# Where the update of T in a blocked triangular inverse is summed: VectorE, or PSUM and ScalarE

## The chip, the cores and the metric

The kernel runs on one core of one Trainium2 chip. The metric is the device time of one execution in microseconds. The engines are TensorE (PE in the profile, its weight loads PEld), VectorE (DVE), ScalarE (ACT), GpSimd (POOL) and SyncE (SP, which here only issues DMAs). Each runs its own instruction list in order.

## The reference, cut to what matters

The program is a whole two-block network (a mixer block with gated DeltaNet and a state-space part, a convolutional feed-forward, then a recurrent and attention block with a mixture of experts). The change is in one piece of the gated delta rule (GDN). Per chunk of tokens, head and direction the reference solves a unit lower triangular system:

```
kk = jnp.einsum('bhnid,bhnjd->bhnij', kb, k) * decay
rhs = jnp.concatenate([v * beta[..., None], kb * jnp.exp(gc)[..., None]], axis=-1)
sol = lax.linalg.triangular_solve(kk, rhs, left_side=True, lower=True, unit_diagonal=True)
u, w = sol[..., :DV], sol[..., DV:]
...
def step(S, inp):
    u_c, w_c, qk_c, qd_c, kd_c, gl_c = inp
    v_new = u_c - jnp.einsum('bhcd,bhde->bhce', w_c, S)
    o_c = jnp.einsum('bhcd,bhde->bhce', qd_c, S) + jnp.einsum('bhij,bhje->bhie', qk_c, v_new)
    S = S * gl_c[..., None, None] + jnp.einsum('bhcd,bhce->bhde', kd_c, v_new)
    return S, o_c
```

## The kernel before

`phase_gdn` works on chunks of 128 tokens, ten chunks (eight of the sequence, two of the context) in two directions: 20 pairs (c, d), four heads each in one tile `[128, 4, 128]`. `prep(c, d, sl)` builds the inverse of a chunk's triangular matrix E. It starts from the identity and goes through seven levels, block sizes s = 1, 2, 4 ... 64 (`for l in range(7)`). T (`Tt`, float16) is the inverse so far, U (`Ut`) its transpose. One level is:

- L577: `pz` = Eh times the half of the columns of T that this level changes (view `Tv`): four matmuls of 64 columns, one for each head.
- L580, VectorE: `Z` = pz times the mask of the level.
- L593: `py` = Ut times Z, four matmuls of 64 columns (at level 0 Ut is the identity and Z itself is used).
- L594, VectorE: `Tv` = Tv minus py, reading PSUM and writing float16 back in place.
- L598 and L599: `put`, the changed rows of the transpose, by four matmuls, copied into `Ut` by ScalarE.

After the levels one refinement (`pn`, `R`, `pd`, L603 to L612) gives U. `step(c, d)` (L618 on) is the recurrence that uses it: float32 matmuls `pa`, `pb`, `pS`, `po`, `po2`, with VectorE (L629, L647, L668) and ScalarE (`vo` L637, `ot` L659) between them. `prep` also computes `pk` (L544) and `pq` (L558) in float32, and ScalarE's exponentials `D` (L502).

Five preps are in work at once (`NS = 5`), each with its own `Tt`, `Ut`, `Z`; the generators are advanced in turn, a part of each at a time. All PSUM results of the stage share seven banks (pool `psG`, tag `b`). The eighth bank is that of `zunits` (L706 on): 16 units of 48 float32r matmuls `zz` (L722), which compute the gates from the hidden states. `zunits` stands behind the GDN in the program, and `phase_ssd` behind it; the framework's scheduler, when the program is built, fixes the order of the instructions on each engine, and puts `zz` matmuls between those of the GDN where it finds room. What isn't done by the end of the GDN is done beside `phase_ssd`. Each half of a unit (24 matmuls) needs one load of 1 MB (`hx`, L719, issued by POOL) into one of two buffers, and a unit ends with a Silu on ScalarE (L725) and a store of `zd`, which the end of the next phase loads again (L877).

Of the kernel before, what the change touches and what calls it, by code (L numbers as in the profile page):

```python
# [10 lines left out]
F16 = mybir.dt.float16  # L11
# [3 lines left out]
AF = mybir.ActivationFunctionType  # L15
ALU = mybir.AluOpType
# [104 lines left out]
class K:  # L121
# [382 lines left out]
    def phase_gdn(self):  # L504
        nc, T = self.nc, self.T
# [6 lines left out]
        lv = self.pool("lvl", 1, ctx=st)  # L512
        lvl = lv.tile([128, 2, 7, 64], F32, name="lvl")
        nc.sync.dma_start(lvl, T["lvl"])
        I16 = lv.tile([128, 4, 128], F16, name="I16")
        nc.vector.tensor_copy(I16, self.I[:, None, :].to_broadcast([128, 4, 128]))
        ps = self.pool("psG", 7, PSUM, ctx=st)
        pr = self.pool("gprep", 2, ctx=st)
        ld = self.pool("gld", 3, ctx=st)
# [3 lines left out]
        def bank(name, dt=F32):  # L523
            return ps.tile([128, 4, 128], dt, name=name, tag="b")
# [4 lines left out]
        def cols(t, c):  # L529
            return t[:, :, c * 128:(c + 1) * 128]  # L530

        def prep(c, d, sl):
            kc = cols(self.kT, c)
            vt = ld.tile([128, 4, 128], F32, name="vt")
            nc.sync.dma_start(vt.rearrange("p h f -> p (h f)"), self.vtd[c])
            kt = ld.tile([128, 4, 128], F32, name="kt", bufs=5)
            nc.sync.dma_start(kt.rearrange("p h f -> p (h f)"), self.ktd[c])
            nc.gpsimd.tensor_tensor(kt, kt, self.erest[:, c, d, 0:4, None].to_broadcast([128, 4, 128]), op=ALU.mult)
            kt_[c, d] = kt
            D = ld.tile([128, 4, 128], F32, name="D")  # L540
            self.rows(D, c, d, 0)
            pk = bank("pk")
            for h in range(4):
                nc.tensor.matmul(pk[:, h, :], kc[:, h, :], kc[:, h, :], start=True, stop=True)  # L544
            yield
            self.expd(D, c, d, 0)
            yield
            E = pr.tile([128, 4, 128], F32, name="E")
            for h in range(4):
                nc.vector.scalar_tensor_tensor(E[:, h, :], pk[:, h, :], self.br2[:, c, d, h:h + 1], D[:, h, :],  # L550
                                               op0=ALU.mult, op1=ALU.mult)
            nc.gpsimd.affine_select(E, E, pattern=[[0, 4], [1, 128]], compare_op=ALU.not_equal, fill=1.0,
                                    base=0, channel_multiplier=-1)
            if c < 8:
                qc = cols(self.qT, c)
                pq = bank("pq")
                for h in range(4):
                    nc.tensor.matmul(pq[:, h, :], kc[:, h, :], qc[:, h, :], start=True, stop=True)  # L558
                P[c, d] = pr.tile([128, 4, 128], F32, name="P", bufs=5)
                nc.vector.tensor_mul(P[c, d], D, pq)  # L560
            yield
            Eh = pr.tile([128, 4, 128], F16, name=f"Eh{sl}", bufs=1)
            nc.scalar.copy(Eh, E)
            Tt = pr.tile([128, 4, 128], F16, name=f"Tt{sl}", bufs=1)
            nc.vector.tensor_copy(Tt, I16)
            Ut = pr.tile([128, 4, 128], F16, name=f"Ut{sl}", bufs=1)
            nc.gpsimd.tensor_copy(Ut, I16)
            yield
            for l in range(7):
                s = 1 << l  # L570
                Tv = Tt.rearrange("p h (n t s) -> p (h n) t s", t=2, s=s)[:, :, d, :]
                Uv = Ut.rearrange("p h (n t s) -> p (h n) t s", t=2, s=s)[:, :, 1 - d, :]
                Iv = I16[:, 0, :].rearrange("p (n t s) -> p n t s", t=2, s=s)[:, :, 1 - d, :]
                pz = ps.tile([128, 4, 64], F32, name="pz", tag="b")
                for h in range(4):
                    r = Tt[:, h, :].rearrange("p (n t s) -> p n t s", t=2, s=s)[:, :, d, :]
                    nc.tensor.matmul(pz[:, h, :].rearrange("p (n s) -> p n s", s=s), Eh[:, h, :], r,  # L577
                                     start=True, stop=True)
                Z = pr.tile([128, 4, 64], F16, name=f"Z{sl}", bufs=1)
                nc.vector.tensor_tensor(Z, pz, lvl[:, d, l, None, :].to_broadcast([128, 4, 64]), op=ALU.mult)  # L580
                if l == 0:
                    El = pr.tile([128, 4, 128], F16, name=f"El{sl}", bufs=1)
                    nc.gpsimd.tensor_tensor(El, E, Eh, op=ALU.subtract)
                    vh = sp.tile([128, 4, 128], F32, name="vh", bufs=5)
                    nc.gpsimd.tensor_tensor(vh, vt, self.rinv[:, c, :, None].to_broadcast([128, 4, 128]), op=ALU.mult)
                    vh_[c, d] = vh
                yield
                if l == 0:
                    y = Z
                else:  # L590
                    y = ps.tile([128, 4, 64], F32, name="py", tag="b")
                    for h in range(4):
                        nc.tensor.matmul(y[:, h, :], Ut[:, h, :], Z[:, h, :], start=True, stop=True)  # L593
                nc.vector.tensor_tensor(Tv, Tv, y.rearrange("p h (n s) -> p (h n) s", s=s), op=ALU.subtract)  # L594
                yield
                put = ps.tile([128, 4, 64], F32, name="put", tag="b")
                for h in range(4):
                    nc.tensor.matmul(put[:, h, :].rearrange("p (n s) -> p n s", s=s), Tt[:, h, :], Iv, start=True, stop=True)  # L598
                nc.scalar.copy(Uv, put.rearrange("p h (n s) -> p (h n) s", s=s))  # L599
                yield  # L600
            pn = bank("pn")
            for h in range(4):
                nc.tensor.matmul(pn[:, h, :], Eh[:, h, :], Tt[:, h, :], start=True, stop=False)  # L603
                nc.tensor.matmul(pn[:, h, :], El[:, h, :], Tt[:, h, :], start=False, stop=True)
            R = pr.tile([128, 4, 128], F16, name="R")
            nc.vector.tensor_tensor(R, Ibc, pn, op=ALU.subtract)
            yield
            pd = bank("pd")
            for h in range(4):
                nc.tensor.matmul(pd[:, h, :], R[:, h, :], Ut[:, h, :], start=True, stop=True)  # L610
            u = pr.tile([128, 4, 128], F32, name="U", bufs=4)
            nc.vector.tensor_tensor(u, Ut, pd, op=ALU.add)  # L612
            U[c, d] = u
# [66 lines left out]
        while ndone < len(order):  # L680
            for d in range(2):
                if cur[d] is None and chains[d] and (chains[d][0], d) in U:
                    cur[d] = step(chains[d].pop(0), d)
                if cur[d] is not None:
                    try:
                        next(cur[d])
                    except StopIteration:
                        cur[d] = None
                        ndone += 1
            rnd += 1  # L690
            if free and nprep < len(order) and nprep < ndone + 6 and rnd >= nxt:
                nxt = rnd + 4
                sl = free.pop(0)
                slots[sl] = prep(*order[nprep], sl)
                nprep += 1
            for sl in list(slots):
                try:
                    next(slots[sl])
                except StopIteration:
                    del slots[sl]  # L700
                    free.append(sl)
# [1522 lines left out]
```

## Time and profile before

| | us |
|---|---|
| median of 3 runs | 3375.71 (3370.09 to 3376.39) |
| the profiled execution | 3373.24 |
| its span | 3371.1 |
| PE busy in the span | 3088.8 (92%) |
| PEld, weight loads | 2327.3 (69%) |
| DVE busy | 1841.7 (55%) |
| ACT busy | 1171.6 (35%) |
| POOL busy | 509.0 (15%) |

What is touched lies in two of 40 slices and a bit: the first level's matmuls start 381 us into the span, the last change of T starts at 617.8 us. Shares over the whole span say little about it. A busy PE in this profile is a stretch in which some matmul was between its start and its modelled end, so the matmuls' durations overlap; how many fit behind each other is read from their starts.

### The profile page before, as it was taken

To read this page: it belongs to the slowest core of one execution; us is meant where nothing else is said; L and a number is where in the kernel's file an instruction comes from. 1 tells how busy PE (TensorE), PEld (TensorE's weight loads), DVE (VectorE), ACT (ScalarE), POOL (GpSimd) and SP (SyncE) were. 2 spreads that over 40 slices of the span, in tenths; PEclk is the share of its full clock that TensorE was granted. 3 is DMA by queue.
4 is the path that set the end of the run, shared out by engine and by line. 5 is a ranking of instruction groups with operands and counts; after the bars stand their busy time and mean duration, and the time that the engine had idled before them with its cause. 6 is when DMAs were issued, how large, how long until landed. Compare 5 with 4: busy or idle time off the path is not lost. (4 is left out here: it accounts for less than half of the span.)

```text
span 3371.1 us, 43138 instructions
## 1 busy us (share of the span) xinstructions
PE 3088.8 (92%) x16679; PEld 2327.3 (69%) x16679; DVE 1841.7 (55%) x3344; ACT 1171.6 (35%) x2568; POOL 509.0 (15%) x416
## 2 busy tenths in 40 slices
PE   7999799877999999999999899999999997988886
PEld 3788689776788888888787787777777784322222
DVE  5754589557666564564778822458886454100000
ACT  4432455544432221122445512237775221111110
POOL 0000355344300000000233200000000101111110
PEclk9999799988999999999999999999999997999999
DMA  6942432786211111111211122200004458999996
GB/s 223 292 133 67 143 127 92 234 288 234 81 58 57 47 50 48 44 50 50 75 51 42 40 75 94 70 32 25 26 14 148 171 189 341 399 399 392 400 396 259
DMA packets 178188, 502.12 MB, mean 149 GB/s; under 512 B 21391, under 2 KB 85519, under 8 KB 148287
## 3 DMA queue, kind: packets, MB, share of 16 engines
q1 hardware_dynamic: 134928, 413.88, 33.5%
q0 software_dynamic: 14832, 52.81, 5.0%
q10 hardware_dynamic: 28223, 32.67, 2.7%
q8 instruction: 132, 2.16, 0.3%
q14 instruction: 73, 0.60, 0.1%
HBM read 450.39 MB, written 67.23 MB: 154 GB/s over the span
## 5 line engine op out<-in xcount | busy, mean ns | idle before, releaser
L2071 PE MATMUL ph<-wraw,xTt 128*64 128x512 f32 x1056 | 283.5, 606 | 49.1 <-DMA wraw<-in_w_dram 45.6
L158 ACT CAST wh<-wf 128x1024 fp32r<-128x1024 f32 x128 | 134.1, 1049 | 531.8 <-PE pg L943 187.2
L941 PE MATMUL pg<-hx,wh 128*128 128x512 f32 (+1 forms) x864 | 263.5, 385 | 8.5 <-DVE xt L1289 6.4
L943 PE MATMUL pg<-hx,wh 128*128 128x512 f32 (+1 forms) x864 | 262.4, 384 | 0.0
L945 PE MATMUL pg<-hx,wl 128*128 128x512 f32 (+1 forms) x864 | 262.1, 384 | 0.0
L2071 PEld LDWEIGHTS ph<-wraw,xTt 128*64 128x64 f32 x1056 | 84.5, 138 | 222.1 <-issue 122.6
L1069 DVE SCALAR_TENSOR_TENSOR acc<-pad,fcw,acc 128x1024 f32<-128x1024 f32 x176 | 226.0, 1284 | 21.3 <-ACT acc L1066 16.8
L159 DVE TENSOR_TENSOR wl<-wf,wh 128x1024 fp32r<-128x1024 f32 x96 | 117.0, 1219 | 136.2 <-ACT wh L158 135.6
L941 PEld LDWEIGHTS pg<-hx,wh 128*128 128x128 f32 x864 | 161.7, 190 | 41.5 <-ACT ainh L158 6.8
L943 PEld LDWEIGHTS pg<-hx,wh 128*128 128x128 f32 x864 | 161.7, 190 | 32.0
L945 PEld LDWEIGHTS pg<-hx,wl 128*128 128x128 f32 x864 | 161.5, 190 | 32.1 <-DVE wl L159 0.3
L722 PE MATMUL zz<-hx 128*128 128x256 f32 x768 | 131.7, 314 | 37.7 <-DMA hx<-hxd 21.0
L2088 PE MATMUL py<-wraw,hT 128*64 128x512 f32 x528 | 150.2, 601 | 3.7 <-issue 2.8
L2074 DVE SCALAR_TENSOR_TENSOR hs<-ph,gate,hs 128x256 f32<-128x256 f32 x32 | 15.5, 484 | 250.7 <-ACT hs L2073 250.7
L722 PEld LDWEIGHTS zz<-hx 128*128 128x128 f32 x768 | 109.2, 207 | 44.4 <-DMA hx<-hxd 15.4
L1027 POOL TENSOR_TENSOR sx<-sx,sqx 128x1024 f32<-128x1024 f32 x7 | 20.2, 2880 | 723.8 <-ACT sqx L1026 723.8
L1105 DVE SCALAR_TENSOR_TENSOR x<-pd,mod,x 128x1024 f32<-128x1024 f32 x42 | 53.9, 1282 | 136.3 <-PE pd L1100 136.3
L2092 DVE COPY yt<-py 128x512 f32<-128x512 f32 x33 | 22.8, 692 | 187.2 <-ACT yt L2091 187.2
L2073 ACT ACTIVATE hs<-ph 128x256 f32<-128x256 f32 x33 | 12.6, 383 | 282.0 <-PE ph L2071 282.0
L159 POOL TENSOR_TENSOR wl<-wf,wh 128x1024 fp32r<-128x1024 f32 x32 | 84.1, 2631 | 138.9 <-ACT wh L158 138.9
L225 PE MATMUL pj<-hxh,wh 128*128 128x512 f32 x320 | 103.4, 400 | 0.0
L225 PE MATMUL pj<-hxl,wh 128*128 128x512 f32 x320 | 102.6, 399 | 0.0
(702 smaller groups left out, 7565.6 us busy)
## 6 DMA issues: line engine op xcount, KB each, us to landing
wraw<-in_w_dram SPq DMA_DIRECT2D x132, 1024.0 KB, 22.3
wraw<-in_w2e_dram SPq DMA_DIRECT2D x66, 1024.0 KB, 22.9
hx<-hxd POOLq DMA_DIRECT2D x32, 1024.0 KB, 7.0
wa<-in_wadaT_dram SPq DMA_DIRECT2D x32, 512.0 KB, 5.0
wf<-in_wgate_dram SPq DMA_DIRECT2D x22, 512.0 KB, 3.2
wf<-in_wup_dram SPq DMA_DIRECT2D x22, 512.0 KB, 3.2
wf<-in_wconv_dram SPq DMA_DIRECT2D x20, 512.0 KB, 3.2
wdf<-in_wdown_dram SPq DMA_DIRECT2D x40, 256.0 KB, 2.6
```

Of the source, the lines that this page charges most:

```text
L158: nc.scalar.copy(hi, x)
L159: (eng or nc.vector).tensor_tensor(lo, x, hi.bitcast(F32), op=ALU.subtract)
L225: nc.tensor.matmul(ps[:, o:o + n], w[:, k, :], (hl if lo else hh)[:, k, ho:ho + n], start=k == 0 and i == 0, stop=k == 7 and i == 2)
L722: nc.tensor.matmul(zz[:, i, :], hx[:, a, k, :], WZ[:, b, k, :], start=k == 0 and j == 0, stop=k == 7 and j == 2)
L941: nc.tensor.matmul(ps[:, o:o + n], wh[:, k, :], xh[:, k, o:o + n], start=k == 0, stop=False)
L943: nc.tensor.matmul(ps[:, o:o + n], wh[:, k, :], xl[:, k, o:o + n], start=False, stop=False)
L945: self.lastmm = nc.tensor.matmul(ps[:, o:o + n], wl[:, k, :], xh[:, k, o:o + n], start=False, stop=k == nk - 1)
L1069: nc.vector.scalar_tensor_tensor(acc, pad[:, dy:dy + 16, dx:dx + 64], cw[:, f, tp:tp + 1], acc, op0=ALU.mult, op1=ALU.add)
L1105: nc.vector.scalar_tensor_tensor(x, pp, self.mod2[:, 24 + m:25 + m], x, op0=ALU.mult, op1=ALU.add)
L2071: nc.tensor.matmul(ph[m], x[:, k, m], f[s][:, j, :], start=k == 0, stop=k == 7)
L2088: nc.tensor.matmul(py[m, o * 512:o * 512 + 512], h[:, j, m], f[s][:, 2 * j + o, :], start=j == 0, stop=j == 1)
L2092: nc.vector.tensor_copy(y[:, 512:1024], py[:, 512:1024])
```

## The change

A tile `N16` (minus the identity, float16) is made once by VectorE. From level 1 on, `py` starts with a product of `N16` with `Tv`, one matmul of 256 columns (64 of each of four heads), and the four products of level and head are added to it in the same PSUM bank. So the bank holds py minus T. ScalarE then writes `Tv` as minus one times the bank, in float16. VectorE's subtraction is left only for level 0.

```diff
         I16 = lv.tile([128, 4, 128], F16, name="I16")
         nc.vector.tensor_copy(I16, self.I[:, None, :].to_broadcast([128, 4, 128]))
+        N16 = lv.tile([128, 128], F16, name="N16")
+        nc.vector.tensor_scalar(N16, self.I, -1.0, None, op0=ALU.mult)
...
                 if l == 0:
-                    y = Z
+                    nc.vector.tensor_tensor(Tv, Tv, Z.rearrange("p h (n s) -> p (h n) s", s=s), op=ALU.subtract)
                 else:
                     y = ps.tile([128, 4, 64], F32, name="py", tag="b")
+                    yv = y.rearrange("p h (n s) -> p (h n) s", s=s)
+                    nc.tensor.matmul(yv, N16, Tv, start=True, stop=False)
                     for h in range(4):
-                        nc.tensor.matmul(y[:, h, :], Ut[:, h, :], Z[:, h, :], start=True, stop=True)
-                nc.vector.tensor_tensor(Tv, Tv, y.rearrange("p h (n s) -> p (h n) s", s=s), op=ALU.subtract)
+                        nc.tensor.matmul(y[:, h, :], Ut[:, h, :], Z[:, h, :], start=False, stop=h == 3)
+                    nc.scalar.activation(Tv, yv, AF.Copy, scale=-1.0)
                 yield
```

## Rows read from the trace of the kernel before

**Rows 1.** Windows: us, then busy PE, PEld, DVE, ACT, POOL; PEclk, DMA share, GB/s.
```profile
480.00:520.00 40.00, 38.69 (x510) 37.89 (x506) 35.43 (x95) 22.97 (x71) 25.34 (x29) 1.00 0.28 88
...
580.00:600.00 20.00, 19.42 (x306) 18.08 (x303) 18.57 (x50) 12.40 (x34) 5.86 (x7) 1.00 0.42 134
...
420.00:620.00 200.00, 191.22 (x2599) 184.12 (x2597) 172.77 (x452) 110.78 (x324) 102.27 (x116) 0.99 0.35 111
626.00:800.00 174.00, 139.77 (x950) 130.27 (x950) 90.47 (x112) 88.04 (x244) 81.12 (x81) 0.91 0.85 285
```

**Rows 2.** Waits of TensorE, 420 to 620 us: waiter, awaited, us, times, longest.
```profile
PE pS L642 <- ACT vo L637: 3.8, 3, 3.0
PE pz L577 <- ACT Eh L563: 2.7, 4, 1.2
PE pb L634 <- DVE vh L629: 1.3, 2, 0.8
PE pd L610 <- DVE R L606: 0.3, 1, 0.3
```

**Rows 3.** Waits of VectorE, 420 to 620 us.
```profile
DVE Tt L594 <- PE py L593: 7.7, 16, 1.8
DVE S L647 <- PE pS L642: 7.3, 10, 3.4
DVE Z L580 <- PE pz L577: 3.1, 4, 1.8
```

**Rows 4.** Waits of ScalarE, 420 to 620 us.
```profile
ACT Ut L599 <- PE put L598: 25.1, 37, 1.8
ACT vo L637 <- PE pb L634: 24.7, 13, 2.9
...
ACT D L502 <- POOL D L497: 9.7, 7, 4.4
```

**Rows 5.** Groups by line, 380 to 626 us, VectorE and ScalarE: busy us, mean ns.
```profile
L580 DVE TENSOR_TENSOR Z<-pz,lvl 128x256 f16<-128x256 f32 x140 | 58.2, 419 | 5.4 <-PE pz L577 5.2
L594 DVE TENSOR_TENSOR Tt<-Tt,py 128x256 f16<-128x256 f16 x120 | 49.7, 416 | 11.0 <-PE py L593 9.8
...
L599 ACT CAST Ut<-put 128x256 f16<-128x256 f32 x140 | 51.9, 387 | 35.2 <-PE put L598 34.9
```

**Rows 6.** Timeline of PE: start us, us from first start to last end, instructions.
```profile
490.35 0.22 PE L604 MATMUL pn<-Tt,El 128*128 128x128 f16 x1
490.40 0.22 PE L603 MATMUL pn<-Tt,Eh 128*128 128x128 f16 x1
490.46 0.22 PE L604 MATMUL pn<-Tt,El 128*128 128x128 f16 x1
...
629.06 3.13 PE L722 MATMUL zz<-hx 128*128 128x256 f32 x24 [0.69 <-ACT zs L725]
```

**Rows 7.** Windows of line 722 alone (zz): us, busy PE, busy PEld.
```profile
480.00:520.00 40.00, 3.81 (x14) 2.29 (x14) 1.00 0.28 88
...
580.00:600.00 20.00, 6.54 (x31) 4.50 (x31) 1.00 0.42 134
...
380.00:626.00 246.00, 49.75 (x227) 33.84 (x227) 0.95 0.35 110
626.00:794.00 168.00, 81.96 (x541) 75.35 (x541) 0.91 0.88 294
```

**Rows 8.** Timeline behind the GDN: zz halves, the last store, its reader.
```profile
635.84 4.62 PE L722 MATMUL zz<-hx 128*128 128x256 f32 x24 [3.21 <-DMA hx<-hxd]
...
650.60 4.62 PE L722 MATMUL zz<-hx 128*128 128x256 f32 x24 [4.14 <-DMA hx<-hxd]
...
797.98 0.38 ACTq L726 DMA_DIRECT2D zd<-zs  x1
...
802.74 1.26 POOL L879 TENSOR_TENSOR hx<-hx,zy 128x512 f32<-128x512 f32 x1 [0.52 <-DMA zy<-zd]
```

**Rows 9.** DMA issues, 620 to 800 us: count, KB each, median us to landing.
```profile
hx<-hxd POOLq DMA_DIRECT2D x21, 1024.0 KB, 7.6
```

**Rows 10.** Timeline of the start of the stage.
```profile
368.99 1.93 DVE L516 CAST I<-cst 128x512 f16<-128x512 f32 x1 [1.17 <-ACT cs L385]
...
380.79 0.40 PE L577 MATMUL pz<-Tt,Eh 128*128 128x64 f16 x4 [15.95 <-ACT Eh L563]
```

## The prediction

> **What bounds the kernel now.** The page's shares over the whole span hide the stage, so I read it by windows first, then who waits for whom inside it, then the lines that the change touches, then what runs behind it. The GDN's level work lies between 381 and 626 us. In its steady part, 420 to 620 us, PE shows 191.2 of 200 us, the weight loads 184.1, DVE 172.8, ACT 110.8 [rows 1]. Two engines look full, and the change takes from one and gives to the other, so everything hangs on which of them sets the pace. The waits tell it. In these 200 us TensorE waited 8.1 us in all, 6.5 for ScalarE and only 1.6 for VectorE [rows 2]. VectorE waited for TensorE: 7.7 us for py, 7.3 for pS, 3.1 for pz [rows 3], and so did ScalarE, 25.1 us for put and 24.7 for pb [rows 4]. So the others stand behind TensorE nearly always, and TensorE behind VectorE almost never. Modelled ends can hide short stalls of TensorE, so I don't take its 96% at its word; but the direction of the waits agrees with it.
>
> There are two kinds of stretch. Where float32 products (pk, pq, the steps) run, as from 480 to 520 us, PE shows 38.7 of 40 and there is room for 14 zz matmuls. Where all five preps are in their levels, as from 580 to 600 us, DVE shows 18.6 of 20 and PE takes 31 zz [rows 1, 7]. The second kind makes up 460 to 480, 520 to 540 and 580 to 600 us, some 60 us of the 200.
>
> Behind the GDN the rest of zz sets the time. 227 matmuls were done by 626 us and 541, that is 11.3 units of 48, from 626 to 794 us: 168 / 11.3 = 14.9 us a unit [rows 7]. 48 matmuls need 2 x 3.13 = 6.3 us of PE [rows 6]; the rest is waiting for the 1 MB loads (3.2 and 4.1 us before a half [rows 8], 7.6 us from issue to landing [rows 9]) in a stretch where the DMA engines are 85% busy [rows 1]. Its end counts: the store of the last unit is issued at 798.0 us, and POOL's L879, which multiplies by such gates, waits for the loads of zd at 802.7 [rows 8]. So a zz matmul costs 0.13 us in the GDN and 14.9 / 48 = 0.31 us behind it.
>
> **The change, part by part.**
>
> *The subtraction leaves VectorE.* 120 instructions at 416 ns, 49.7 us [rows 5]. Of this the path gets what TensorE waited for VectorE: 1.6 us in the 200 [rows 2], 2 us over the stage; the most would be what VectorE gains in the second kind of stretch, taken up in the rivals. I take 2.
>
> *The product with N16.* 120 matmuls of 256 float16 columns, with a weight load each. No such row exists. Float16 matmuls of 128 columns, each with its own weights, start 0.055 us after each other (490.35, .40, .46), so 256 columns take about 0.11; the zz of 256 columns give 24 in 3.13 us, 0.13 each with the last one's end in it [rows 6]. Sum 120 x 0.11 = 13.2 us, at most 120 x 0.13 = 15.6, at least nothing where it lies in a stall of TensorE (the matmul needs only T, not Z, so it can run while Z is made; but the order is fixed beforehand, and a place in a stall isn't sure). I take 13.2, since TensorE's idle time in the stretch is small and zz already fills it. The Trainium skill (TensorE: Matmul & The Clock Gate, section Back-to-back issue gap) gives N/2.4 + 2.5 ns for a lone gap, 109 ns at 256 columns, but about 81 ns at 128 columns and 131 at 512 in a stream with weight loads; by the stream's figures 256 columns would be some 95 ns, an estimate, and the sum 11.4 us. The rows at 128 columns show 55 ns, so the stream's figure doesn't hold here.
>
> *ScalarE writes T.* 120 more instructions of the shape of L599's, 387 ns each, 46.4 us [rows 5]. In the 200 us that is about 99 x 0.387 = 38 on top of 110.8, 149 of 200: not full. What is behind the write on ScalarE's queue are copies of Ut, vo, ot, exponentials; what waits for it is put of the same level and pz of the next, on TensorE. Before, ScalarE's part (Ut) was needed only one product later (py of the next level); now T, on which both following products wait, stands in ScalarE's queue. That queue has stalls of its own: 9.7 us for POOL's D, up to 4.4 us in one piece, and 24.7 for pb [rows 4]. VectorE's queue had fewer (7.3 us for pS) but was fuller. Bounds: a loss of the 9.7 us if every such stall is handed on to TensorE, a gain of the 1.6 us of VectorE's waits that is already counted; five preps in work give TensorE other products in between, so I take nothing.
>
> *Banks.* py's bank is now taken from the N16 product on, before Z is there, instead of from the first product with Z: longer by about Z's 0.42 us [rows 5] of seven banks, 120 times, 50 of 7 x 246 bank-microseconds. Nothing, or at most as much as the product itself if a bank is short then. N16 itself, one VectorE operation on a quarter of L516's 1.93 us, lies in the 16 us in which TensorE waits for the first Eh [rows 10]: nothing, and 0.5 us if it didn't.
>
> *zz.* With TensorE fuller, the scheduler finds less room. I take it that the stage grows by TensorE's work and zz keeps its 227. The other end: the second kind of stretch, with about 100 zz in 60 us [rows 7], shortens because VectorE is relieved, and those zz are pushed back. That is 100 x 0.13 = 13 us less in the stage and 100 x 0.31 = 31 more behind it, net 18 slower.
>
> Sum: +13.2 - 2 = +11 us on the profiled execution's 3373.2 (span 3371.1 and 2.1 around it) gives 3384. That execution lies 2.5 us under the median of the three, so on the median it would be 3387; I name 3385.
>
> **The rivals.**
>
> *VectorE sets the pace (faster).* In the stretches of the second kind DVE is 93% busy [rows 1] and half its work there is pairs of Z and T. With T gone a pair of 0.42 + 0.42 us becomes 0.42, and TensorE, which there holds some 4 us of zz in 20, has the room. If the 60 us become 45 and zz still finds its places between (also in the 8 us in which TensorE waited), the stage ends 15 us earlier, N16 included: 3373.2 - 15 = 3358. For it: DVE's share, and VectorE's queue at 86% delays every Z. Against: TensorE's waits. It decides if more than about 13 us of TensorE's time from 381 to 626 us is really stall. The Trainium skill (Perfetto Trace Analysis, section Identifying the Most-Contended Engine) would not judge TensorE by matmul busy time but by weight loads, and the others by occupancy: from 480 to 520 us that names TensorE (37.9 to 35.4 of 40), from 580 to 600 VectorE (18.6 to 18.1 of 20), so by it the second kind should gain [rows 1].
>
> *Hidden anyway (no change).* The 13.2 us lie in stalls of TensorE that the modelled ends hide, and VectorE's relief pays the rest: 3368 to 3380.
>
> *zz is pushed back (slower still).* As worked out, 13.2 - 2 + 18 = +29: 3402. For it: zz is put only where room is left, and costs 0.31 us behind the GDN. Against: SSD's work could fill some of those waits.
>
> **How the numbers follow.** Forecast (3379 to 3392) 0.35, VectorE sets the pace 0.28, hidden 0.22, zz pushed back 0.15. A change under 0.2%, 6.8 us, can't be told from none. Part of the forecast's case lies inside that: faster 0.28, same 0.26, slower 0.46. The likeliest case's own range is 3379 to 3392; the range that holds the time 8 in 10 leaves out the far half of the faster and of the pushed-back case: 3357 to 3404.
>
> **What would show it.** L594 keeps 20 instructions, a new ScalarE line has 120 at 0.37 to 0.40 us, L593's place has 120 float16 matmuls of 256 columns whose successors start 0.11 us later. Right: in the stage PE stays over 95% busy, VectorE falls to about 130 of 200 us with its waits for TensorE grown, and the last change of T comes 5 to 13 us later than 617.8. zz's count up to the end of the GDN tells the third rival. Wrong: the last change of T comes over 10 us earlier with 200 or more zz done by then, or zz behind the GDN takes clearly less than 14.9 us a unit, so that its being pushed back costs nothing.

## The result, and the profile after

The changed kernel is slower: 3407.1 us (3405.6 to 3410.0, four runs) against 3373.9 us beside it, a ratio of 1.0098 (95% interval 1.0086 to 1.0110). The profiled execution took 3405.6 us with a span of 3403.8, 32.7 more than before. The forecast was 3385 with a range that ended at 3404: the direction was right, the size was not, and the time lies 3 us outside the range.

The windows of [rows 1] for the changed kernel (columns as there):

```profile
480.00:520.00 40.00, 39.36 (x526) 37.80 (x525) 32.46 (x82) 26.87 (x91) 23.38 (x28) 1.00 0.26 81
580.00:600.00 20.00, 19.99 (x320) 19.03 (x319) 13.72 (x34) 13.57 (x46) 2.32 (x2) 1.00 0.10 28
420.00:620.00 200.00, 191.01 (x2632) 182.09 (x2631) 142.29 (x358) 130.91 (x426) 98.45 (x110) 1.00 0.24 76
626.00:800.00 174.00, 137.28 (x910) 126.53 (x911) 86.66 (x113) 85.15 (x215) 76.24 (x75) 0.89 0.82 280
```

In the steady 200 us VectorE fell from 172.8 to 142.3, ScalarE rose from 110.8 to 130.9, and TensorE shows 191.0 as before. In 580 to 600 us VectorE fell from 18.6 to 13.7 of 20, and TensorE rose to 19.99. Who waits for whom, 420 to 620 us (waiter, awaited, us, times, longest), one fence, TensorE's rows first; they answer to [rows 2 to 4]:

```profile
PE pS L646 <- ACT vo L641: 3.2, 3, 1.2
PE put L602 <- ACT Tt L598: 1.8, 4, 0.8
PE pb L638 <- DVE vh L633: 1.4, 2, 0.9
...
DVE S L651 <- PE pS L646: 15.6, 16, 2.3
DVE Z L582 <- PE pz L579: 11.9, 21, 1.7
DVE U L616 <- PE pd L614: 11.8, 14, 1.2
...
ACT vo L641 <- PE pb L638: 23.4, 15, 3.8
ACT Tt L598 <- PE py L597: 14.8, 14, 1.5
ACT Ut L603 <- PE put L602: 11.2, 19, 1.7
```

TensorE's waits stay small, VectorE's waits for TensorE at S and at Z are two and four times what they were: TensorE sets the pace as before, and part of the time that VectorE was given went into waiting. The last change of T is earlier, not later, than its 617.8 us before (instruction, count, ns min/median/max, first and last start in us):

```profile
L598 ACT ACTIVATE Tt<-py x120: 364/396/470, 391.0 to 610.6; 128x256 f16<-128x256 f32 x120
```

So the GDN became quicker and the kernel slower. Three instructions show where the loss is: the last tile of the recurrence's output (L672, before L668; it marks the end of the GDN), the last Silu of a gate unit (L729, before L725), and the first product of the phase that needs everything (`pw` in `phase_mix`, L984, before L980). First the kernel before, then after:

```profile
L668 DVE TENSOR_TENSOR hx<-ot,po x16: 677/682/690, 465.1 to 628.7; 128x512 f32<-128x512 f32 x16
L725 ACT ACTIVATE zs<-zz x16: 597/597/598, 444.1 to 793.4; 128x512 f32<-128x512 f32 x16
L980 PE MATMUL pw<-hx,wh x128: 387/389/792, 832.7 to 881.7; 128*128 128x512 f32 x128
```

```profile
L672 DVE TENSOR_TENSOR hx<-ot,po x16: 677/679/687, 462.5 to 621.6; 128x512 f32<-128x512 f32 x16
L729 ACT ACTIVATE zs<-zz x16: 577/597/598, 522.5 to 835.2; 128x512 f32<-128x512 f32 x16
L984 PE MATMUL pw<-hx,wh x128: 387/389/761, 864.0 to 910.4; 128*128 128x512 f32 x128
```

The GDN ends 7.1 us earlier (628.7 to 621.6), the last gate comes 41.8 us later, and `pw` starts 31.3 us later; behind it the two kernels run alike (span +32.7). What lies between is zz. Windows of its line alone, to and from the end of the GDN (us, busy PE, busy PEld, PEclk, DMA share, GB/s), before and after:

```profile
380.00:628.70 248.70, 51.54 (x240) 35.45 (x240) 0.95 0.35 111
628.70:793.40 164.70, 80.17 (x528) 73.74 (x528) 0.91 0.88 297
```

```profile
380.00:621.60 241.60, 21.03 (x96) 14.48 (x96) 0.96 0.26 83
621.60:835.20 213.60, 104.37 (x672) 95.63 (x672) 0.89 0.83 283
```

Before, 240 of the 768 zz matmuls were done by the end of the GDN; after, 96. Each one behind it costs about the same in both: 164.7 / 528 = 0.312 us and 213.6 / 672 = 0.318. So the account is -7.1 us for the GDN, 213.6 - 164.7 = +48.9 for the zz behind it, and the way from the last gate to `pw` shrank from 39.3 to 28.8 us, -10.5: together +31.3.

### The profile page after: what moved, and what is told of

It reads as the page before. It is cut to its first block, busy times and chain, and to the rows that moved or that the text cites. A ratio compares the mean times of both kernels' runs of the same rounds, so it can differ in the third digit from the quotient of the medians.

```text
span 3403.8 us, 43429 instructions
## 1 busy us (share of the span) xinstructions
PE 3104.8 (91%) x16799; PEld 2337.5 (69%) x16799; DVE 1803.1 (53%) x3225; ACT 1200.3 (35%) x2686; POOL 511.5 (15%) x416
## 3 DMA queue, kind: packets, MB, share of 16 engines
q1 hardware_dynamic: 134928, 413.88, 33.2%
## 5 line engine op out<-in xcount | busy, mean ns | idle before, releaser
L1073 DVE SCALAR_TENSOR_TENSOR acc<-pad,fcw,acc 128x1024 f32<-128x1024 f32 x176 | 225.9, 1284 | 21.3 <-ACT acc L1070 16.8
```

The lines of the kernel that those rows point to most:

```text
L1073: nc.vector.scalar_tensor_tensor(acc, pad[:, dy:dy + 16, dx:dx + 64], cw[:, f, tp:tp + 1], acc, op0=ALU.mult, op1=ALU.add)
```

## The experiments

The theories: **A**, what decides is how many zz matmuls are placed within the GDN; each that falls behind it costs some 0.3 us there and gives back 0.13. **B**, the write of T in ScalarE's queue delays the levels. **C**, TensorE's added work is all, through the GDN's length. **D**, the work beside zz behind the GDN (`phase_ssd`) has a length of its own, so that fewer zz there help only down to a point.

All twelve kernels and the two under comparison, sorted by the zz matmuls left behind the GDN. "By PE's work" is a sum, not a measurement: 628.7 us, plus 13.2 where the 120 products with N16 are in it, plus 0.13 for each zz more than 240 within the GDN (less for fewer). Times are starts in the profiled execution, as above; the ratios are those of the timed runs.

| kernel | ratio to before (95%) | zz in / behind | GDN end | by PE's work | last gate | `pw` | GDN end to `pw` |
|---|---|---|---|---|---|---|---|
| b_pin4 | 1.0008 (0.9992 to 1.0023) | 446 / 322 | 654.9 | 655.5 | 755.1 | 843.9 | 189.0 |
| a_pin4 | 1.0075 (1.0053 to 1.0096) | 446 / 322 | 669.6 | 668.7 | 774.5 | 859.0 | 189.4 |
| b_pin3 | 1.0029 (1.0016 to 1.0041) | 337 / 431 | 644.2 | 641.3 | 797.6 | 845.4 | 201.2 |
| b_pin25 | 0.9975 (0.9965 to 0.9985) | 288 / 480 | 638.4 | 634.9 | 793.6 | 834.8 | 196.4 |
| **before** | 1 | 240 / 528 | 628.7 | | 793.4 | 832.7 | 204.0 |
| b_pin2 | 0.9992 (0.9980 to 1.0004) | 238 / 530 | 625.4 | 628.4 | 804.0 | 837.4 | 212.0 |
| a_pin2 | 1.0029 (1.0016 to 1.0042) | 235 / 533 | 637.2 | 641.2 | 796.8 | 834.8 | 197.6 |
| b_extra | 1.0078 (1.0060 to 1.0095) | 169 / 599 | 634.8 | 632.7 | 840.0 | 868.6 | 233.8 |
| a_noprod | 1.0049 (1.0033 to 1.0066) | 144 / 624 | 617.3 | 616.2 | 834.7 | 863.7 | 246.4 |
| **after** | 1.0098 (1.0086 to 1.0110) | 96 / 672 | 621.6 | 623.2 | 835.2 | 864.0 | 242.4 |
| a_noload | 1.0109 (1.0088 to 1.0130) | 96 / 672 | 622.8 | 623.2 | 800.4 | 833.2 | 210.4 |
| b_late | 1.0164 (1.0143 to 1.0185) | 0 / 768 | 617.9 | 597.5 | 860.2 | 889.6 | 271.7 |
| b_zz0 | 1.0101 (1.0083 to 1.0119) | 32 zz in all | 651.8 | | 736.2 | 879.2 | 227.4 |
| a_zz0 | 0.9938 (0.9915 to 0.9961) | 32 zz in all | 659.0 | | 686.9 | 818.9 | 159.9 |

Names with a_ start from the changed kernel, with b_ from the kernel before. A zz matmul counts as in the GDN when it starts before the GDN's end. Three things are read from the table. In the kernels with all of zz and all loads the way from the GDN's end to `pw` is 189 to 201 us up to 480 zz behind the GDN, 198 to 212 about 530, and grows beyond: from before's 528 to b_late's 768 by 67.7 us, 0.28 for each. In b_extra, a_noprod, after and b_late, with most zz behind the GDN, `pw` follows the last gate by 28.6 to 29.4 us; before it took 39.3, so there the last gate alone didn't decide. And the profile of before is one execution of 3373.2 us, low among its runs (the medians beside the experiments are 3378.3 to 3381.0), so a distance to its marks is up to 8 us too long; the ratios go by the runs beside each kernel. The changed kernel itself was timed only beside the 3373.9 us; against the medians beside the experiments its 3407.1 us would be 26 to 29 us longer instead of 33.

**b_extra: the product alone.** The kernel before, with N16 and a product of it with Tv whose result is overwritten by the `py` products; VectorE keeps the subtraction.

```diff
...
                     y = ps.tile([128, 4, 64], F32, name="py", tag="b")
+                    nc.tensor.matmul(y.rearrange("p h (n s) -> p (h n) s", s=s), N16, Tv, start=True, stop=True)
```

> The kernel before with one more product of N16 with T ahead of each py, overwritten by py's own matmuls: TensorE's part of the change alone, 120 x 0.11 = 13 us, nothing taken from VectorE. Theory A (what counts is how many zz matmuls are done when the GDN ends; each one later costs 0.31 us there): fewer than 227 zz by the GDN's end and +10 to +30 us. Theory B (ScalarE's queue delays T): no more than TensorE's own 13 us and zz's place kept, 0 to +13. Theory C (TensorE's added work is all of it): about +33, as in the changed kernel.

Measured 3407.6 us against 3381.0, 26.6 longer: within A's range, over B's and short of C's 33. The GDN's end moves by 6.1 us, and 71 zz move out of it (window of zz to the GDN's end, columns as above):

```profile
380.00:634.80 254.80, 38.55 (x169) 26.91 (x170) 0.96 0.28 89
```

`pw` comes 35.9 us later, and the GDN's length is only 6.1 of that, so it isn't C's road; the rest lies in the zz behind it.

**a_noprod: ScalarE's write alone.** The changed kernel without the product, so T isn't in the sum and its values, and what depends on them, are wrong.

```diff
-                    nc.tensor.matmul(yv, N16, Tv, start=True, stop=False)
                     for h in range(4):
-                        nc.tensor.matmul(y[:, h, :], Ut[:, h, :], Z[:, h, :], start=False, stop=h == 3)
+                        nc.tensor.matmul(y[:, h, :], Ut[:, h, :], Z[:, h, :], start=True, stop=True)
```

> The changed kernel without the N16 product (T is left out of the sum, so T becomes minus the update alone): ScalarE's part of the change alone. Theory A: the relief of VectorE makes the levels shorter and so takes room from zz; the GDN ends 10 to 20 us earlier, 50 to 110 fewer zz are done by then, total 0 to +20. Theory B: +20 to +33, with the GDN ending no earlier than before. Theory C: 0 or faster.

3397.8 us against 3381.0 (the profiled execution, 3402.5, is the longest of its four). The windows of zz (columns as above):

```profile
380.00:617.30 237.30, 31.62 (x144) 21.73 (x144) 0.96 0.32 94
617.30:834.80 217.50, 97.83 (x624) 89.39 (x624) 0.84 0.79 268
```

With the subtraction moved and no work added to TensorE, the GDN ends 11.4 us earlier, which 96 zz fewer in it explain (96 x 0.13 = 12.5), and `pw` still starts 31.0 us later than before. B wanted a later GDN and is out; C wanted no loss and is out; by the medians the loss, 16.8 us, is half of the changed kernel's 33.2, without its product. A's three numbers came in. The order of zz on TensorE is fixed when the program is built: by the order of starts in the traces 217 zz stand ahead of the last `pn` before, 144 in b_extra, 123 in a_noprod, 75 after. Either half of the change makes the scheduler put them later, by 73 and 94; both together, by 142.

**b_zz0 and a_zz0: 736 of the 768 zz matmuls left out** (gates are wrong), the loads kept, to see the GDN without zz.

```diff
-                    for k in range(8):
-                        for j, (a, b) in enumerate(((0, 0), (0, 1), (1, 0))):
-                            nc.tensor.matmul(zz[:, i, :], hx[:, a, k, :], WZ[:, b, k, :],
-                                             start=k == 0 and j == 0, stop=k == 7 and j == 2)
+                    nc.tensor.matmul(zz[:, i, :], hx[:, 0, 7, :], WZ[:, 1, 7, :], start=True, stop=True)
```

> The kernel before with 32 of the 768 zz matmuls (one for each half, the rest left out; loads and stores stay). It is the base of a_zz0. All theories: faster than before by 20 to 120 us, since the loads run early.

> The changed kernel with the same 32 of 768 zz matmuls. Against b_zz0, Theory A: no slower, 0 to -15 us, since there is nothing left that could be pushed back. Theory B: +5 to +30 us, since T still waits in ScalarE's queue. Theory C: about +13 us.

All theories missed in both: b_zz0 was to be faster than before, and a_zz0 came 58 us under b_zz0, more than any of them had. With nearly all of zz gone the kernel before took 3416.6 us against 3381.0, **longer**, and its GDN ended at 651.8. The single matmul left in each half still waits, in TensorE's order, for its load (TensorE's waits behind the GDN, 655 to 880 us):

```profile
PE zz L720 <- DMA hx<-hxd: 41.0, 11, 6.3
...
PE zz L720 <- ACT zs L722: 14.2, 3, 9.5
```

and the granted clock fell with the busy time (windows of all engines as above; first the kernel before, then b_zz0):

```profile
460.00:500.00 40.00, 38.58 (x531) 37.34 (x531) 33.70 (x94) 21.77 (x64) 19.71 (x23) 0.96 0.35 114
```

```profile
380.00:420.00 40.00, 20.81 (x268) 17.99 (x269) 24.69 (x68) 18.66 (x54) 20.70 (x25) 0.66 0.47 158
460.00:500.00 40.00, 31.32 (x441) 29.84 (x439) 29.46 (x81) 22.52 (x61) 16.86 (x21) 0.85 0.45 155
660.00:700.00 40.00, 6.00 (x13) 3.45 (x13) 5.04 (x9) 9.45 (x40) 4.78 (x9) 0.50 1.03 365
```

An experiment that takes a filler out but leaves its waits measures the waits. For A against B it says nothing. That a_zz0 ran 1.7% faster than b_zz0 comes mostly from the same waits: of the 32 matmuls 27 stand in the GDN in a_zz0, and only 14 in b_zz0. Windows of zz to the GDN's end, first b_zz0, then a_zz0, and a_zz0's waits for loads behind it (659 to 819 us):

```profile
380.00:651.80 271.80, 5.54 (x14) 3.09 (x14) 0.89 0.39 129
```

```profile
380.00:659.00 279.00, 9.04 (x27) 4.89 (x27) 0.90 0.55 178
```

```profile
PE zz L724 <- DMA hx<-hxd: 5.7, 3, 2.6
```

Behind the GDN TensorE waited 5.7 us for loads instead of 41.0, and `pw` follows the GDN's end by 159.9 us instead of 227.4. Why both GDNs end later than with zz in them (651.8 and 659.0) isn't explained.

**a_pin2 and b_pin2: the same zz in both.** `zunits` yields after each matmul, and the GDN's loop of 129 rounds takes two from round 20 on, so that its place is written by hand.

```diff
+        zu = self.zunits(psz, zp)
...
+            if rnd >= 20:
+                for _ in range(2):
+                    next(zu, None)
...
-        self.zunits(psz, zp)
+        for _ in zu:
+            pass
...
+                            yield
```

> The changed kernel with zunits as a generator that the GDN's loop advances by two zz matmuls in each round from round 20 on, so that about as many (some 220) are done when the GDN ends as in the kernel before. Theory A: the GDN ends 8 to 17 us later than in the changed kernel (630 to 639), the rest of zz takes 0.31 to 0.34 us each, total +0 to +15 us against before, 15 to 30 less than the changed kernel. Theory B (the delay is in T's way through PSUM and ScalarE): +25 to +35 us, as the changed kernel.

> The kernel before with the same two zz matmuls a round. Theory A: the same count as before, -5 to +10 us. Theory B says nothing of it.

With zz held in place the changed kernel's loss falls from 0.98% to 0.29% (3387.5 us), and b_pin2 is at the kernel before (3378.5 against 3378.9). The ends in a_pin2, then in b_pin2:

```profile
L672 DVE TENSOR_TENSOR hx<-ot,po x16: 674/679/689, 467.3 to 637.2; 128x512 f32<-128x512 f32 x16
L735 ACT ACTIVATE zs<-zz x16: 575/597/599, 454.4 to 796.8; 128x512 f32<-128x512 f32 x16
```

```profile
L668 DVE TENSOR_TENSOR hx<-ot,po x16: 673/678/689, 463.0 to 625.4; 128x512 f32<-128x512 f32 x16
L731 ACT ACTIVATE zs<-zz x16: 574/597/600, 418.0 to 804.0; 128x512 f32<-128x512 f32 x16
```

The GDN's ends lie 11.8 us apart, near the 13.2 of the 120 products, and the medians 9.0. The profiled executions themselves differ less (spans 3376.1 and 3376.9): that of a_pin2 was the shortest of its ten, which go from 3377.9 to 3395.5, and its `pw` comes 2.6 us before that of b_pin2, so the medians decide. By them the change without its side effect is slower by 9 us here, near the forecast's sum of +11, and B's +25 to +35 is out; the next pair gives more.

**a_pin4 and b_pin4: four a round.**

> The changed kernel with four zz matmuls a round, some 420 done when the GDN ends. Theory A: the GDN ends 20 to 45 us later than in the changed kernel, 320 fewer are left at 0.31 us each (100 us): total 15 to 40 us under before. A rival (D: behind the GDN it is not zz but the state-space part that sets the end, so zz's place is worth little): no faster than with two a round.

> The kernel before with four a round. Theory A: 15 to 40 us under before, and within 10 us of the changed kernel with four a round, since then zz's place is the same in both; the changed one slower by at most TensorE's added 13 us. Theory B: the changed one slower by 20 us or more. Theory D: as with two a round.

A's 15 to 40 us under before missed in both: a_pin4 took 3401.9 us and b_pin4 3382.1, 23.0 and 3.2 us over the 3378.9 beside them. D's forecast, no faster than with two a round, came in. 446 zz are in the GDN, which grows as TensorE's work says (a_pin4, then b_pin4):

```profile
L672 DVE TENSOR_TENSOR hx<-ot,po x16: 673/680/687, 471.5 to 669.6; 128x512 f32<-128x512 f32 x16
```

```profile
L668 DVE TENSOR_TENSOR hx<-ot,po x16: 674/679/689, 469.2 to 654.9; 128x512 f32<-128x512 f32 x16
```

Here the change itself costs 19.8 us by the medians, twice what it cost with two a round; A had allowed 13, and B began at 20. In the profiled executions the GDN ends 14.7 us later, near the 13.2 of the products, and `pw` comes 15.1 later, so no delay of T beyond TensorE's work is seen in the GDN; where the remaining 5 us lie stays open.

In b_pin4 the last gate is ready at 755.1, 38 us earlier than before. `pw` isn't: it starts at 843.9, 189.0 us behind the GDN, and in a_pin4 189.4. All engines of b_pin4, to the last gate and from it to `pw`:

```profile
654.90:755.10 100.20, 72.74 (x487) 67.69 (x486) 41.09 (x53) 51.62 (x153) 38.52 (x40) 0.88 0.93 316
755.10:843.90 88.80, 60.03 (x295) 50.69 (x295) 73.05 (x142) 32.82 (x91) 50.76 (x38) 0.75 0.52 168
```

For 88.8 us behind the last gate VectorE works 73.1 on `phase_ssd`. That fits D, and it bounds A; but D's length isn't fixed at 189 us, since a_zz0, with five zz matmuls behind the GDN, needed 159.9.

**b_late: no zz in the GDN.** Two small copies of the GDN's last output into the two load buffers make the first loads, and so all zz, wait for its end.

```diff
+        for i in range(2):
+            nc.vector.tensor_copy(HX[:, i, :, :, 0], self.oacc[:, 7 - 7 * i, 0, 0:16].rearrange("p (a k) -> p a k", a=2))
```

> The kernel before with every zz held back until the GDN is done (two small copies from the GDN's last outputs into the buffers of the loads). By the line of the runs so far the GDN ends 240 x 0.13 = 31 us earlier (near 597 us), and 768 zz at 0.31 to 0.34 us take 238 to 261 us: last Silu at 835 to 860, total +35 to +65 us. Theory D (the state-space part sets the end): -20 to +10 us.

3431.2 us against 3378.3, the slowest of all, as A had it and D hadn't: all 768 lie behind the GDN, from 617.9 to 860.2 us, 0.316 each. The GDN's own end missed, at 617.9, 20 us later than TensorE's work says: without zz its products don't fill TensorE (windows of all engines):

```profile
420.00:600.00 180.00, 161.37 (x2242) 152.52 (x2242) 159.32 (x423) 91.91 (x289) 92.27 (x103) 0.97 0.20 59
```

So it takes the filler for TensorE to set the GDN's pace; without it TensorE and VectorE are busy nearly alike, and what sets its end there isn't shown.

**a_noload: 24 of the 32 loads left out** (`if c0 == 0:` ahead of the `dma_start` of `hx`; gates are wrong), to see whether the loads make the 0.31 us.

> The changed kernel with 8 of the 32 loads of hx (only the first pair of each quarter of the columns; the other units reuse what is there, so these gates are wrong). If the price of a zz behind the GDN is the wait for its load, it falls from 0.32 towards TensorE's own 0.13 us, the last Silu comes before 760 us, and the total is 25 to 50 us under the changed kernel, until the state-space part's own 190 us behind the GDN set the end. If the price is TensorE or the Silu, no more than 10 us under the changed kernel.

The wrong gates send the tokens through one expert pass more, so the total (3413.0 us) isn't comparable, and I read it at `pw`: 833.2 us against 864.0, 30.8 less. The last gate comes at 800.4, later than the expectation had it, and a zz matmul behind the GDN takes 177.7 / 672 = 0.264 us instead of 0.318. TensorE's waits of zz behind the GDN, in the changed kernel (622 to 835 us) and in this one (625 to 800):

```profile
PE zz L726 <- DMA hx<-hxd: 31.0, 14, 7.2
```

```profile
PE zz L727 <- ACT hx L158: 5.6, 3, 3.0
PE zz L727 <- DMA hx<-hxd: 4.7, 2, 3.5
PE zz L727 <- ACT zs L730: 3.7, 3, 1.8
```

So the waits for loads are 26 us less, and that would be most of the 31. Even so the price is twice the 0.13 of a zz within the GDN; I put the rest down to the state-space part on the same in-order engine, which no run separates.

**b_pin25 and b_pin3: a mean of 2.5 and 3 a round, on the kernel before.**

> The kernel before with two and three zz matmuls a round in turn, some 290 done when the GDN ends (near 634 us). Behind it 478 zz x 0.32 + 39 = 192 us and the state-space part's 189 are even there, so this is where the two lines cross: -4 to -10 us against before. By Theory D alone: 0 to +5.

> The kernel before with three a round, some 340 done when the GDN ends (near 640 us); the state-space part's 189 us set the end: -5 to +3 us against before.

b_pin25 beats both kernels, by as much as forecast: 3368.4 us against 3378.3, 0.9975 (0.9965 to 0.9985). b_pin3, at 3387.5, is 9.2 us slower than before and missed its forecast: 49 zz more in the GDN cost 19 us, where 0.13 each makes 6, and b_pin4, with 446 in it, is back at +3.2. So A and D together don't give these totals, and that the optimum lies where the two meet isn't shown. What stays open, too: the profiled execution of b_pin25 (3372.9 us) is the second longest of its twelve and that of before a short one, and its `pw` comes 2.1 us later than before's, so where the 10 us come from isn't seen.

## Why the prediction was wrong

**That TensorE sets the pace** of the GDN held where zz fills it. The column "by PE's work" meets the measured end within about 4 us in the ten kernels that have 96 or more zz in the GDN, with no term for VectorE at all. In a_noprod VectorE has 120 subtractions less and nothing is put on TensorE, and the end moves only by the zz that left. The 2 us that I gave to the subtraction aren't to be seen. The rival in which VectorE sets the pace is refuted where zz is held alike: a_pin2 has VectorE relieved and ends its GDN 11.8 us after b_pin2. b_late, with no zz in the GDN, ends 20 us later than TensorE's work, so there TensorE doesn't set it. The rule of the Trainium skill (Perfetto Trace Analysis, section Identifying the Most-Contended Engine), by which VectorE bound the stretches of the second kind, isn't borne out: from 580 to 600 us VectorE fell by a quarter, and what changed at the end of the GDN is covered by zz leaving it.

**The product at 0.11 us** held. Timeline of TensorE in the changed kernel (start us, us to the last end):

```profile
500.26 0.28 PE L595 MATMUL py<-Tt,N 128*128 128x256 f16 x1
500.38 0.28 PE L597 MATMUL py<-Z,Ut 128*128 128x64 f16 x4
500.49 0.28 PE L579 MATMUL pz<-Tt,Eh 128*128 128x64 f16 x4
```

The successor starts 0.12 us later, and the GDN's ends give 11.8 us for 120 in a_pin2 against b_pin2 and 14.7 in a_pin4 against b_pin4, where I had 13.2.

**ScalarE's write at nothing** held nearly. An instruction takes 396 ns in the median for the 387 taken. Its bound was 9.7 us; from 380 to 626 us TensorE waited 3.0 us for the new T (1.8 of it after 420, in the waits above), its weight loads 5.7, and TensorE 3.1 for Ut:

```profile
PEld L602 <- ACT Tt L598: 5.7, 12, 1.0
...
PE py L597 <- ACT Ut L603: 3.1, 1, 3.1
PE put L602 <- ACT Tt L598: 3.0, 8, 0.8
```

The ends of the GDN leave no room for more.

**The step that failed is "I take it that the stage grows by TensorE's work and zz keeps its 227."** By the GDN's end 96 were done, where the kernel before had 240 (227 by 626 us). The other end, some 100 pushed back, stood in the same paragraph and as the third rival (3402 us, chance 0.15), and that is what happened, with 144 instead of 100. I had its two prices right: 0.31 us behind the GDN (0.318 after), and 0.13 within it. With the true count the sum comes out at 144 x (0.31 - 0.13) = 26, and 13.2 for the product, +39; the way from the last gate to `pw` gave 10.5 back, which leaves +29 of the measured +31.3 (the GDN's end, 7.1 us earlier, is in it: 13.2 - 144 x 0.13 = -5.5 by these prices). That last term was in no case of mine: the final gate isn't alone in deciding when `pw` starts, as the table and b_pin4 show.

Its cause in the rival was too narrow as well. I had zz pushed out because stretches relieved of VectorE shorten. a_noprod fits this (96 fewer), but b_extra, with VectorE's work left as it was, loses 71. What both halves have in common is, I take it, that they change what the scheduler reckons with when it orders TensorE's list; the order itself shows where zz went (the zz ahead of the last `pn`), but why the scheduler put them there stays open.

**The signs that I named.** TensorE over 95% (95.5) came out; VectorE fell, but to 142.3 of 200 us and not to 130; "the last change of T comes 5 to 13 us later" came out with the other sign, 7.2 earlier, for the same reason as the failed step: less zz in the stage. The count of zz was named as what tells the third rival, and it did.

## What to carry to other kernels

Where work without a deadline fills an engine's gaps, price a change by where that filler goes, at its cost in the place that it is pushed to; here the change cost 9 and 20 us in the two pairs with the filler held, and 26 to 33 without, by which runs of the kernel before it is taken against. A stage that ends earlier is no gain if it left work behind: read the next point at which everything must be ready. And where a scheduler places the filler, count it in the engine's list before believing that it stays, and pin it by hand before comparing two versions of the work around it.

## What the runs showed of the hardware that I had not expected

- Taking matmuls away can lower the clock that TensorE is granted. In b_zz0 the granted clock was 0.66 in the mean from 380 to 420 us and 0.85 from 460 to 500, between its two levels of 1.2 and 2.4 GHz (0.50 and 1.00), where the kernel before had 0.73 and 0.96; from 660 to 700 us, with 6.0 of 40 us busy, it stood at 0.50. TensorE had been less busy in each of these stretches. How much of the 36 us (3416.6 against 3381.0) is the clock and how much the bare waits for loads wasn't separated. The lower clock alone doesn't make the kernel slower: a_zz0 had 0.68 and 0.91 in the first two stretches and ran 22.5 us faster than before (3358.5 against 3381.0).
